# S5 scan: the states of both halves in one tile, both advanced by one VectorE operation, the second half some steps behind

## The chip, the core and the metric

The kernel runs on one core of one Trainium2 chip. Each time is in device microseconds (us) for the whole program. A core has TensorE (PE, matrix products; PEld is its weight load), VectorE (DVE), ScalarE (ACT), GpSimd (POOL) and SyncE (SP, which issues nearly all transfers), and 16 DMA engines that move data between the chip's main memory (DRAM) and its on-chip memory.

## The reference

Two layers over 2048 latent tokens with 256 context tokens in front. The first layer (state space and windowed attention) is not touched. The second is a bidirectional S5 layer: a complex diagonal recurrence along the sequence, with 64 groups of 16 channels, 64 states each, once forwards and once backwards; the context's last state is where the latent part starts.

```python
def s5_scan(u, ab_re, ab_im, bb_re, bb_im, h0_re, h0_im):
    bu_re = jnp.einsum('blgc,gnc->blgn', u, bb_re)
    bu_im = jnp.einsum('blgc,gnc->blgn', u, bb_im)
    ...
    _, _, h_re, h_im = lax.associative_scan(combine, (a_re, a_im, bu_re, bu_im), axis=1)
    return h_re, h_im

def s5_bidir(u, disc, init):
    hf_re, hf_im = s5_scan(u, *disc[0], *init[0])
    hb_re, hb_im = s5_scan(jnp.flip(u, axis=1), *disc[1], *init[1])
    final = [(hf_re[:, -1], hf_im[:, -1]), (hb_re[:, -1], hb_im[:, -1])]
    return hf_re + jnp.flip(hb_re, axis=1), hf_im + jnp.flip(hb_im, axis=1), final

def odd_layer(...):
    u, g = jnp.split(norm_mod(x, norm_w, shift, scale) @ w_in, 2, axis=-1)
    ...
    y = s5_output(s_re, s_im, ug, c_re, c_im, d_skip, glu_w, glu_b) * jax.nn.silu(g)
    x = x + gate * (y @ w_out)
```

## The kernel before

The sequence is cut into 144 blocks of 16 tokens: 16 context blocks, then 128 latent ones. Within a block everything is a matrix product; only the state at the block's edge is carried from block to block. The S5 layer therefore has four parts that run beside each other:

- **odd_proj** (matmuls into tile `mm`, by `mm3` at lines 312 to 314) projects the tokens. Its first blocks give `u`, which goes to DRAM as `u_d` (line 1835), 144 columns per row: 16 of context, 128 of latent. Its later blocks give the gate `g`: ScalarE makes `tz` (line 1849), VectorE `uev` (line 1850). The `mm` tile has two buffers, so TensorE can be at most two tiles ahead of line 1850.
- **s5_in** loads `u_d` (tile `U`, line 1891) and, for each of 64 groups, multiplies it into `ips` (line 1913); ScalarE copies this into `Bu` (lines 1915 and 1916). Groups 0 to 31 are half 0 and fill tile `Bu0`, groups 32 to 63 are half 1 and fill `Bu1`. Each tile is [128, complex part, direction, 16, 145].
- **s5_scan** runs on VectorE alone: 143 steps for each half, each step four dependent operations on 128 x 64 elements (lines 1942, 1943, 1945, 1947), that read and write one slot of `Bu` per state. Forward and backward direction go through the slots in opposite order. Half 0 starts when its input is there; once half 1 has its input too, each step does both halves, eight operations, interleaved. A copy (line 1958) puts the backward start state into slot 144.
- **s5_out** copies the states of a group into `hs` (ScalarE line 1995, forward; GpSimd line 1993, backward) and multiplies (`ops`, lines 2017 and 2019, eight matmuls per group, 512 in all), with `Uo`, `oo` and `ki` loaded from DRAM.

After that **glu** does the last two products. Its first matmuls also run between the last ones of s5_out.

TensorE runs in the order in which the program is written out. A planner (`merge`, `turn`) writes it: it keeps a count `pe` of planned TensorE time, and a generator that yields `("until", t)` or `("wait", x)` is taken up again when `pe` has passed `t`, or `x` is done. The scan charges `SCP` = 0.73 us per half and step, so its pace in that plan fixes where the first matmul of s5_out stands among those of odd_proj. The other engines' order is set by a scheduler; each engine runs its own list in order.

Of the kernel before, what the change touches and what calls it, by code (L numbers as in the profile page):

```python
# [55 lines left out]
def dap(t, off, dims):  # L56
    return bass.AP(tensor=t.tensor, offset=t.offset + off, ap=[list(d) for d in dims])
# [198 lines left out]
class Net:  # L256
# [75 lines left out]
    def scratch(self):  # L332
# [18 lines left out]
        self.x1_d = s("x1_d", [L, D])  # L351
        self.u_d = s("u_d", [64, 16, 16, 144])
        self.g2_d = s("g2_d", [D, LX])
# [1150 lines left out]
    def s5_gen(self, e):  # L1504
# [3 lines left out]
        c = self.const  # L1508
        self.AR = c.tile([P, 2, 32], F32, name="AR")
        self.AI = c.tile([P, 2, 2, 32], F32, name="AI")  # L1510
        cp = e(self.pool("g_c", bufs=1, side="right"))
# [90 lines left out]
        V.tensor_scalar(nq, pw[:, 1, :, :, 8], -1.0, None, op0=ALU.mult)  # L1602
        V.tensor_copy(self.AR, pn[:, 0, 16, :].rearrange("p (a b) -> p a b", a=2))
        V.tensor_scalar(self.AI[:, 0], pn[:, 1, 16, :].rearrange("p (a b) -> p a b", a=2), -1.0, None, op0=ALU.mult)
        V.tensor_copy(self.AI[:, 1], pn[:, 1, 16, :].rearrange("p (a b) -> p a b", a=2))

# [142 lines left out]
    def odd_proj(self):  # L1749
# [69 lines left out]
        def ublk(ch, b):  # L1819
            o = {}  # L1820

            def evac(ci, ps):
                if ci == 0:
                    o["e"] = vp.tile([P, TT], F32, name="uev")
                out = o["e"][:, ci * 256:ci * 256 + ps.shape[-1]]
                if ch[ci] == 0:

                    out = out.rearrange("p (s j) -> p s j", s=16)
                    ps = bass.AP(tensor=ps.tensor, offset=ps.offset + 15, ap=[list(ps.ap[0]), [-1, 16], [16, 16]])
                A.activation(out, ps, AF.Copy)  # L1830

            def end():
                c0, cl = ch[0] == 0, [c for c in ch if c]
                for (q, n, j, S0, j0) in [(0, 16, 16, 0, 0)] * c0 + [(256 * c0, 2 * len(cl), P, 2 * cl[0] - 2, 16) for _ in cl[:1]]:
                    nc.sync.dma_start(dap(self.u_d, b * 8 * 256 * 144 + S0 * 144 + j0, [[16 * 144, P], [144, n], [1, j]]),
                                      o["e"][:, q:q + n * j].rearrange("p (s j) -> p s j", j=j))
# [40 lines left out]
    def s5_in(self, e):  # L1877

        nc = self.nc
        V, G, A, T = nc.vector, nc.gpsimd, nc.scalar, nc.tensor  # L1880
        NJ = 144
        bp = e(self.pool("s5b", bufs=1, side="right"))

        self.Bu = Bu = [bp.tile([P, 2, 2, 16, NJ + 1], F32, name=f"Bu{h}") for h in range(2)]
        self.sp5 = e(self.pool("s5s", bufs=2, side="right"))
        with ExitStack() as st:
            wk = st.enter_context(self.pool("s5i", bufs=2, side="right"))
            pp = st.enter_context(self.pool("s5p", bufs=4, space=PSUM, side="right"))
            def load(g0):
                u = wk.tile([P, 4, 2, NJ], F32, name="U", bufs=3)  # L1890
                nc.sync.dma_start(u.rearrange("p g b t -> p g (b t)"), dap(self.u_d, g0 * 256 * NJ, [[2 * NJ, P], [256 * NJ, 4], [1, 2 * NJ]]))
                return u

            def load_g(g):
# [4 lines left out]
            for g in range(64):  # L1899
                if g % 4 == 0:  # L1900
                    for g0 in ((0, 4) if g == 0 else (g + 4,)):
                        if g0 < 64:
# [8 lines left out]
                for d in range(2):  # L1911
                    for kb in range(2):
                        T.matmul(ps[:, d, :], lhsT=gv[:, d, kb, :], rhs=u[:, g % 4, kb, :], start=kb == 0, stop=kb == 1)
                par = slice((g % 2) * 64, (g % 2) * 64 + 64)
                A.activation(Bu[g // 32][par, 0, :, g // 2 % 16, 0:NJ], ps[0:64], AF.Copy)
                A.activation(Bu[g // 32][par, 1, :, g // 2 % 16, 0:NJ], ps[64:128], AF.Copy)
                if g % 32 == 31:
# [4 lines left out]
    def s5_scan(self):  # L1922

        V, NJ = self.nc.vector, 144
        def slots(k):
            return k, (15 - k if k < 16 else 159 - k)

        def hv(Bu, k, swap=False):
            f, b = slots(k)
            base = Bu[:, 0, 0, :, 0]  # L1930
            W = NJ + 1
            cst = 2 * 16 * W
            part = [list(x) for x in base.ap][0]
            return bass.AP(tensor=base.tensor, offset=base.offset + f + (cst if swap else 0),
                           ap=[part, [-cst if swap else cst, 2], [16 * W + b - f, 2], [W, 16]])
# [12 lines left out]

        k = [1, 1]
        yield ("wait", ("in", 0))  # L1950
        t = self.pe
        while min(k) < NJ:
            w = [h for h in range(2) if k[h] < NJ and ("in", h) in self.done]
            step([(h, k[h]) for h in w])
            for h in w:
                k[h] += 1
                if k[h] == NJ:
                    V.tensor_copy(self.Bu[h][:, :, 1, :, NJ], self.Bu[h][:, :, 1, :, 0])
                    self.done.add(("scan", h))
            t += SCP * len(w)  # L1960
            yield ("until", t)

    def s5_out(self, e):
# [10 lines left out]
        def load(g):  # L1974
            if g % 2 == 0:
                U = wk.tile([P, 2, 2, NJ], F32, name="Uo", bufs=UB)
                nc.sync.dma_start(U.rearrange("p g b t -> p g (b t)"), dap(self.u_d, g * 256 * NJ, [[2 * NJ, P], [256 * NJ, 2], [1, 2 * NJ]]))
                oo = wk.tile([P, 2, 2, 256], F32, name="oo", bufs=UB)
# [21 lines left out]
        for g in range(64):  # L2000
# [245 lines left out]
```

## Time and profile before

| | |
|---|---|
| median of 3 runs | 3734.67 us (3730.95 to 3739.14) |
| the profiled execution: its time, its span | 3735.82 us, 3734.0 us |
| TensorE busy | 3405.1 us, 91% |
| VectorE busy | 2437.0 us, 65% |
| ScalarE, GpSimd busy | 1652.1 us (44%), 1142.7 us (31%) |
| mean granted TensorE clock, share of full | 0.961 |

Busy shares are means over the whole program; what counts for a change is the stage in which it lies. The S5 scan runs from 2919 to 3215 us.

### The profile page before, as it was taken

Reading aid. Unit: us, or ns where it says so; the run is one execution under the profiler, and the core shown is the slowest. Engines: PE = TensorE matmul, PEld = TensorE weight load, DVE = VectorE, ACT = ScalarE, POOL = GpSimd, SP = SyncE. Lnnn points to the kernel's source line nnn. Section 1 sums busy time; section 2 is a strip of 40 time slices with the busy share of each in tenths; the row PEclk is TensorE's granted clock in tenths of the full one; section 3 lists DMA queues with packets and bytes.
Section 4 is the critical chain, followed back from the end, with each engine's and each line's share of the span. In section 5 each row is a group of like instructions: output and inputs, shape, how many; then the busy total and the mean of one; then the engine's idle time right before and its main releaser. Section 6 shows DMA issues by size and latency. Waiting matters only on the chain.

```text
span 3734.0 us, 63256 instructions
## 1 busy us (share of the span) xinstructions
PE 3405.1 (91%) x22805; PEld 2938.9 (79%) x22805; DVE 2437.0 (65%) x5671; ACT 1652.1 (44%) x3567; POOL 1142.7 (31%) x754
## 2 busy tenths in 40 slices
PE   6879899998999998789999999988899979989999
PEld 4767788877887887668778888767688868879977
DVE  5887876565535444767677777798782699404455
ACT  4545445443422222667677775244343512343321
POOL 3221234432212332366676652210101111133121
PEclk9999999999999999899999999999899989989999
DMA  8766477875666776665545443568888844895453
GB/s 291 222 213 196 165 235 251 275 243 192 233 229 220 258 255 213 187 192 148 148 131 137 119 114 110 177 190 255 260 255 271 294 157 165 273 279 169 129 165 113
DMA packets 668004, 758.97 MB, mean 203 GB/s; under 512 B 77147, under 2 KB 529691, under 8 KB 667691
## 3 DMA queue, kind: packets, MB, share of 16 engines
q1 hardware_dynamic: 667691, 754.93, 64.3%
q8 instruction: 180, 2.95, 0.3%
q14 instruction: 133, 1.09, 0.1%
HBM read 517.62 MB, written 237.15 MB: 202 GB/s over the span
## 4 chain that ended last, share of the span: by engine, by line
PE 28%; DVE 13%; DMA 8%; SPq 2%; issue 2%; ACT 2%; POOL 1%; DVEq 0%; ACTq 0%; POOLq 0%
PE pv L1217 3%; PE pt L1207 3%; PE mm L312 2%; PE mm L313 2%; PE mm L314 2%; PE S L1187 2%; PE gpo L312 2%; PE gpo L314 2%; PE gpo L313 2%; DVE sc L1942 1%; PE S L1189 1%; DVE Bu L1947 1%; DVE sc L1945 1%; DVE sc L1943 1%; PE f L312 1%
## 5 line engine op out<-in xcount | busy, mean ns | idle before, releaser
L312 PE MATMUL mm<-xTh,wh 128*128 128x256 f32 (+2 forms) x2344 | 840.1, 358 | 71.1 <-DVE uev L1850 24.7
L313 PE MATMUL mm<-xTl,wh 128*128 128x256 f32 (+2 forms) x2344 | 783.3, 334 | 1.3 <-POOL xTl L297 0.7
L314 PE MATMUL mm<-xTh,wl 128*128 128x256 f32 (+2 forms) x2344 | 783.1, 334 | 0.8 <-DVE wl L297 0.8
L312 PEld LDWEIGHTS mm<-xTh,wh 128*128 128x128 f32 (+1 forms) x2344 | 452.3, 193 | 136.2 <-issue 48.2
L313 PEld LDWEIGHTS mm<-xTl,wh 128*128 128x128 f32 (+1 forms) x2344 | 451.8, 193 | 53.9 <-issue 14.7
L314 PEld LDWEIGHTS mm<-xTh,wl 128*128 128x128 f32 (+1 forms) x2344 | 450.3, 192 | 44.2 <-DVE wl L297 1.0
L1211 DVE TENSOR_TENSOR tl<-pt,th 128x512 fp32r<-128x512 f32 x328 | 224.3, 686 | 117.8 <-ACT th L1210 115.3
L1200 DVE TENSOR_SCALAR_CACHE_REDUCE p<-S,nsink 128x640 f32<-128x640 f32 (+2 forms) x288 | 235.3, 820 | 82.0 <-PE S L1189 79.4
L1201 ACT ACTIVATE p<-p,nm 128x640 f32<-128x640 f32 (+2 forms) x288 | 223.9, 778 | 74.7 <-DVE p L1200 72.7
L1210 ACT ACTIVATE th<-pt 128x512 fp32r<-128x512 f32 x328 | 193.8, 592 | 129.8 <-PE pt L1207 126.2
L1207 PE MATMUL pt<-ident,p 128*128 128x128 f32 x1312 | 203.6, 277 | 36.9 <-DVE tl L1211 16.7
L312 PE MATMUL mm<-wh,xTh 128*128 128x256 f32 x720 | 218.9, 304 | 18.8 <-DMA wh<-wk 9.5
L1207 PEld LDWEIGHTS pt<-ident,p 128*128 128x128 f32 x1312 | 156.8, 142 | 72.1 <-issue 22.2
L313 PE MATMUL mm<-wl,xTh 128*128 128x256 f32 x720 | 207.4, 288 | 0.7 <-DMA wl<-wk 0.7
L314 PE MATMUL mm<-wh,xTl 128*128 128x256 f32 x720 | 207.0, 288 | 0.0
L979 DVE SCALAR_TENSOR_TENSOR rf<-rb,s_P,rf 128x128 f32<-128x128 f32 x288 | 139.2, 528 | 94.2 <-ACT rf L975 90.0
L645 DVE SCALAR_TENSOR_TENSOR cA<-cR,vecs,cA 128x256 f32<-128x256 f32 (+3 forms) x192 | 179.2, 945 | 25.5 <-ACT cA L642 20.9
L424 POOL TENSOR_TENSOR xin<-xin,shr 128x1024 f32<-128x1024 f32 x33 | 86.9, 2641 | 303.1 <-DVE xin L423 298.2
L312 PEld LDWEIGHTS mm<-wh,xTh 128*128 128x128 f32 x720 | 141.7, 197 | 25.8 <-DVE zt L602 10.9
L297 POOL TENSOR_TENSOR wl<-w,wh 128x1024 fp32r<-128x1024 f32 (+1 forms) x43 | 100.3, 2335 | 187.1 <-ACT wh L305 187.0
L911 POOL TENSOR_TENSOR xw<-xs,s_de 128x1024 f32<-128x1024 f32 x36 | 72.1, 2003 | 254.4 <-DMA xs<-xs_d 169.5
L601 ACT ACTIVATE tz<-mm 128x256 f32<-128x256 f32 x144 | 53.9, 377 | 216.1 <-PE mm L314 201.7
(466 smaller groups left out, 9064.9 us busy)
## 6 DMA issues: line engine op xcount, KB each, us to landing
wh<-wk SPq DMA_DIRECT2D x116, 512.0 KB
wl<-wk SPq DMA_DIRECT2D x116, 512.0 KB
wk<-wh SPq DMA_DIRECT2D x56, 512.0 KB
wk<-wl SPq DMA_DIRECT2D x56, 512.0 KB
w<-in_e_w_in_dram SPq DMA_DIRECT2D x40, 512.0 KB
xin<-in_x_dram SPq DMA_DIRECT2D x38, 512.0 KB
rf<-prow_d SPq DMA_DIRECT2D x72, 256.0 KB
rb<-prow_d SPq DMA_DIRECT2D x72, 256.0 KB
```

The lines of the kernel that those rows point to most:

```text
L297: eng.tensor_tensor(out, x, hi.bitcast(F32), ALU.subtract)
L312: mm(ps, lhsT=ah, rhs=bh, start=first, stop=False)
L313: mm(ps, lhsT=ah, rhs=bl, start=False, stop=False)
L314: mm(ps, lhsT=al, rhs=bh, start=False, stop=last)
L645: nc.vector.scalar_tensor_tensor(acc[:, q:q + m], R[:, s + j:s + j + m], cw[:, 12 * j + b:12 * j + b + 1], acc[:, q:q + m], op0=ALU.mult, ...
L979: V.scalar_tensor_tensor(rf[:, h], rb[:, h], self.s_P[:, c, 16 + hh:17 + hh], rf[:, h], op0=ALU.add, op1=ALU.min)
L1200: V.tensor_scalar(p[:, :w], s, -0.125, nsink[:, h:h + 1], op0=ALU.mult, op1=ALU.min, accum_out=nm)
L1201: A.activation(p[:, :w], p[:, :w], AF.Exp, bias=nm, scale=-1.0, accum_out=d["sm"][:, h:h + 1])
L1207: T.transpose(pt[:, n, :], Ps[h4][:, j * P:(j + 1) * P], self.ident)
L1210: A.activation(th, pt, AF.Copy)
L1211: V.tensor_tensor(tl, pt, th.bitcast(F32), ALU.subtract)
L1217: T.matmul(pv, lhsT=VV[kt][:, hk, :], rhs=t.rearrange("p a b -> p (a b)"), start=first and x == 0, stop=last and x == 1)
```

## The change

Both halves' states get one tile `Bu` [128, half, complex part, direction, 16, 144]. The backward direction is stored in the order in which its scan runs, so that both directions stand at slot k in step k: the input matmuls of direction 1 read `U` backwards (step -1 along the row), and the copies of direction 1 into `hs` read `Bu` backwards. For this each row of `u_d` carries the context twice, in front and behind (160 columns, one more transfer for each block of `u`), and `U` is loaded in 32 transfers of two groups instead of 16 of four. The copy into slot 144 is gone. `AR` and `AI` are laid out by half.

The scan has three stretches: half 0 alone until half 1's input is there (`lag` steps), then both in one operation per line, on 128 x 128 elements, with half 1 `lag` slots behind, then half 1 alone. The plan charges a joint step 1.5 x SCP where it charged 2 x SCP.

```diff
-        self.u_d = s("u_d", [64, 16, 16, 144])
+        self.u_d = s("u_d", [64, 16, 16, 160])
...
-                for (q, n, j, S0, j0) in [(0, 16, 16, 0, 0)] * c0 + [(256 * c0, 2 * len(cl), P, 2 * cl[0] - 2, 16) for _ in cl[:1]]:
+                for (q, n, j, S0, j0) in [(0, 16, 16, 0, 0), (0, 16, 16, 0, 144)] * c0 + [(256 * c0, 2 * len(cl), P, 2 * cl[0] - 2, 16) for _ in cl[:1]]:
...
-        self.Bu = Bu = [bp.tile([P, 2, 2, 16, NJ + 1], F32, name=f"Bu{h}") for h in range(2)]
+        self.Bu = Bu = bp.tile([P, 2, 2, 2, 16, NJ], F32, name="Bu")
...
-                u = wk.tile([P, 4, 2, NJ], F32, name="U", bufs=3)
+                u = wk.tile([P, 2, 2, NU], F32, name="U", bufs=4)
...
+            def steps(u, d):
+                return u[:, 0:NJ] if d == 0 else bass.AP(tensor=u.tensor, offset=u.offset + NU - 1, ap=[list(u.ap[0]), [-1, NJ]])
...
-                        T.matmul(ps[:, d, :], lhsT=gv[:, d, kb, :], rhs=u[:, g % 4, kb, :], start=kb == 0, stop=kb == 1)
+                        T.matmul(ps[:, d, :], lhsT=gv[:, d, kb, :], rhs=steps(u[:, g % 2, kb, :], d), start=kb == 0, stop=kb == 1)
...
-        def step(halves):
-            t = {}
-            for h, k in halves:
-                t[h] = [self.sp5.tile([P, 2, 2, 16], F32, name=n, bufs=2) for n in ("sc1", "sc2")]
-                ps = slice(h * 16, h * 16 + 16)
-                V.tensor_tensor(t[h][0], hv(self.Bu[h], k - 1), self.AR[:, None, :, ps].to_broadcast([P, 2, 2, 16]), ALU.mult)
-                V.tensor_tensor(t[h][1], hv(self.Bu[h], k - 1, True), self.AI[:, :, :, ps], ALU.mult)
-            for h, k in halves:
-                V.tensor_tensor(t[h][0], t[h][0], hv(self.Bu[h], k), ALU.add)
-            for h, k in halves:
-                V.tensor_tensor(hv(self.Bu[h], k), t[h][0], t[h][1], ALU.add)
+        def at(h, n, k, lag, swap=False):
+            b = self.Bu[:, h, 0, 0, 0, 0]
+            return bass.AP(tensor=b.tensor, offset=b.offset + k + (C if swap else 0),
+                           ap=[list(b.ap[0]), [-C if swap else C, 2], [2 * C - lag, n], [NJ, 32]])
+
+        def step(h, n, k, lag=0):
+            sh = [P, 2, n, 32]
+            t = [self.sp5.tile([P, 2, 2, 32], F32, name=x, bufs=2)[:, :, 0:n] for x in ("sc1", "sc2")]
+            w = lambda a: a.rearrange("p h d q -> p h (d q)")[:, h:h + n]
+            V.tensor_tensor(t[0], at(h, n, k - 1, lag), w(self.AR)[:, None].to_broadcast(sh), ALU.mult)
+            V.tensor_tensor(t[1], at(h, n, k - 1, lag, True), self.AI.rearrange("p c h d q -> p c h (d q)")[:, :, h:h + n], ALU.mult)
+            V.tensor_tensor(t[0], t[0], at(h, n, k, lag), ALU.add)
+            V.tensor_tensor(at(h, n, k, lag), t[0], t[1], ALU.add)
...
+        t, k = self.pe, 1
+        while k < NJ and ("in", 1) not in self.done:
+            step(0, 1, k)
+            k += 1
+            t += SCP
+            yield ("until", t)
+        yield ("wait", ("in", 1))
+        t = max(t, self.pe - 2.0)
+        lag = k - 1
+        while k < NJ:
+            step(0, 2, k, lag)
+            k += 1
+            t += 1.5 * SCP
+            yield ("until", t)
+        self.done.add(("scan", 0))
+        for k in range(NJ - lag, NJ):
+            step(1, 1, k)
+            t += SCP
+            yield ("until", t)
+        self.done.add(("scan", 1))
...
-                    src = Bu[p0 // 16][par * 64:par * 64 + 64, k, d, p0 % 16, (15, 17)[d]:(15, 17)[d] + P]
+                    src = Bu[par * 64:par * 64 + 64, p0 // 16, k, d, p0 % 16, 15:15 + P]
+                    if d:
+                        src = bass.AP(tensor=src.tensor, offset=src.offset + P - 1, ap=[list(src.ap[0]), [-1, P]])
```

How the change moves instructions: TensorE's order is the same in both kernels up to the place where s5_out begins. Before, that is after 1368 units of odd_proj (a unit is one matmul with 256 columns; one with 512 counts as two), all of them counted from the first matmul of s5_in:

```order
L314 MATMUL mm_33752<-xTh_25428,wl_33472 128x256
L2017 MATMUL ops_33837<-Uo_33812,ki_33816 128x128 x2
L2019 MATMUL ops_33837<-hs_33826,oo_33814 128x128 x2
L2017 MATMUL ops_33837<-Uo_33812,ki_33816 128x128 x2
L2019 MATMUL ops_33837<-hs_33826,oo_33814 128x128 x2
```

In the changed kernel the same matmuls (lines 2030 and 2032 there) stand behind 1152 units, after the `mm` tile 33136:

```order
L314 MATMUL mm_33136<-xTh_25428,wl_32920 128x256
L2030 MATMUL ops_33220<-Uo_33195,ki_33199 128x128 x2
L2032 MATMUL ops_33220<-hs_33209,oo_33197 128x128 x2
L2030 MATMUL ops_33220<-Uo_33195,ki_33199 128x128 x2
L2032 MATMUL ops_33220<-hs_33209,oo_33197 128x128 x2
L2030 MATMUL ops_33237<-Uo_33195,ki_33201 128x128 x2
```

So 216 units have moved from in front of the first matmul of s5_out to behind it. Further on, odd_proj's 1800th and last unit stands after 260 of the 512 s5_out matmuls before, after 312 now.

VectorE's list before, at the last step of half 0 (`Bu0`), with the gate evacuation of `mm` tile 33615 three and a half joint steps ahead of it, and that of tile 33668 right behind one step of half 1 alone:

```order
L1850 SCALAR_TENSOR_TENSOR uev_33640<-tz_33641,mm_33615 128x256
L1945 TENSOR_TENSOR sc1_33723<-sc1_33723,Bu0_30427 128x64
...
L1947 TENSOR_TENSOR Bu0_30427<-sc1_33793,sc2_33794 128x2x2x16
L1947 TENSOR_TENSOR Bu1_30428<-sc1_33797,sc2_33798 128x2x2x16
L1942 TENSOR_TENSOR sc1_33891<-Bu1_30428,AR_25075 128x64
L1943 TENSOR_TENSOR sc2_33892<-Bu1_30428,AI_25076 128x64
L1945 TENSOR_TENSOR sc1_33891<-sc1_33891,Bu1_30428 128x64
L1947 TENSOR_TENSOR Bu1_30428<-sc1_33891,sc2_33892 128x2x2x16
L1850 SCALAR_TENSOR_TENSOR uev_33640<-tz_33717,mm_33668 128x256
```

The same list now, from the evacuation of tile 33136 (the last `mm` tile ahead of s5_out on TensorE) to the first step of half 1 alone; the rows left out are twelve joint steps like those shown:

```order
L1854 SCALAR_TENSOR_TENSOR uev_33161<-tz_33162,mm_33136 128x256
L1949 TENSOR_TENSOR sc1_32951<-sc1_32951,Bu_30435 128x128
L1950 TENSOR_TENSOR Bu_30435<-sc1_32951,sc2_32952 128x2x2x32
...
L1947 TENSOR_TENSOR sc1_33125<-Bu_30435,AR_25075 128x128
L1948 TENSOR_TENSOR sc2_33126<-Bu_30435,AI_25076 128x128
L1949 TENSOR_TENSOR sc1_33125<-sc1_33125,Bu_30435 128x128
L1950 TENSOR_TENSOR Bu_30435<-sc1_33125,sc2_33126 128x2x2x32
L1947 TENSOR_TENSOR sc1_33165<-Bu_30435,AR_25075 128x2x32
```

Before, `mm` tiles 33668 and 33752 still stand on TensorE between the tile that is evacuated last and s5_out; now none does, and thirteen and a half joint steps stand behind that evacuation. Up to the end of half 0's scan there were 66 steps of half 0 alone, 77 joint ones and 43 evacuations by line 1850; now there are 65, 78 and 37. Half 1 alone took 66 steps and takes 65.

## Rows read from the trace of the kernel before

**Rows 1.** Busy time by stretch: start:end, length, then as the header names them.

```profile
core 0: us, PE busy (x) PEld busy (x) DVE busy (x) ACT busy (x) POOL busy (x), PEclk, DMA share, GB/s
2975.00:3000.00 25.00, 17.55 (x85) 14.82 (x84) 24.07 (x110) 5.41 (x14) 2.38 (x1) 0.80 0.70 225
...
3275.00:3300.00 25.00, 16.21 (x93) 15.30 (x94) 2.99 (x3) 11.83 (x22) 8.65 (x13) 0.74 1.03 310
```

**Rows 2.** What TensorE waited for, 2900 to 3260: total us, times, longest.

```profile
PE mm L312 <- DVE uev L1850: 24.7, 12, 7.5
PE tp L431 <- DVE xTl L297: 6.7, 8, 2.0
```

**Rows 3.** VectorE in order of time, one step of half 0 alone: start, us.

```profile
2963.55 0.26 DVE L1942 TENSOR_TENSOR sc<-Bu,AR 128x64 f32<-128x64 f32 x1
2963.73 0.25 DVE L1943 TENSOR_TENSOR sc<-Bu,AI 128x64 f32<-128x64 f32 x1
2963.90 0.26 DVE L1945 TENSOR_TENSOR sc<-sc,Bu 128x64 f32<-128x64 f32 x1
2964.19 0.27 DVE L1947 TENSOR_TENSOR Bu<-sc,sc 128x64 f32<-128x64 f32 x1
2964.50 0.26 DVE L1942 TENSOR_TENSOR sc<-Bu,AR 128x64 f32<-128x64 f32 x1
```

**Rows 4.** VectorE in order of time, a joint step, and one with an evacuation.

```profile
3102.94 0.40 DVE L1947 TENSOR_TENSOR Bu<-sc,sc 128x64 f32<-128x64 f32 x2
3103.25 0.27 DVE L1942 TENSOR_TENSOR sc<-Bu,AR 128x64 f32<-128x64 f32 x1
3103.43 0.26 DVE L1943 TENSOR_TENSOR sc<-Bu,AI 128x64 f32<-128x64 f32 x1
3103.61 0.26 DVE L1942 TENSOR_TENSOR sc<-Bu,AR 128x64 f32<-128x64 f32 x1
3103.78 0.26 DVE L1943 TENSOR_TENSOR sc<-Bu,AI 128x64 f32<-128x64 f32 x1
3103.96 0.45 DVE L1945 TENSOR_TENSOR sc<-sc,Bu 128x64 f32<-128x64 f32 x2
3104.33 0.41 DVE L1947 TENSOR_TENSOR Bu<-sc,sc 128x64 f32<-128x64 f32 x2
3104.63 0.26 DVE L1942 TENSOR_TENSOR sc<-Bu,AR 128x64 f32<-128x64 f32 x1
...
3109.91 0.42 DVE L1850 SCALAR_TENSOR_TENSOR uev<-tz,mm 128x256 f32<-128x256 f32 x1
3110.24 0.27 DVE L1943 TENSOR_TENSOR sc<-Bu,AI 128x64 f32<-128x64 f32 x1
```

**Rows 5.** VectorE operations on rows without gaps, grouped by shape: busy us, mean ns.

```profile
L1336 DVE TENSOR_TENSOR ab<-af,ab 128x64 f32<-128x64 f32 x16 | 3.4, 214 | 2.1 <-PE af L388 2.0
...
L1590 DVE TENSOR_TENSOR pn<-pn,pt 128x128 f32<-128x128 f32 x1 | 0.3, 283 | 0.0
```

**Rows 6.** TensorE in order of time: [idle before it <-releaser].

```profile
2992.10 0.76 PE L312 MATMUL mm<-xTh,wh 128*128 128x512 f32 x1 [7.45 <-DVE uev L1850]
...
3118.04 0.47 PE L312 MATMUL mm<-xTh,wh 128*128 128x512 f32 x1 [0.70 <-DVE uev L1850]
...
3144.91 0.60 PE L2017 MATMUL ops<-Uo,ki 128*128 128x128 f32 x4
3145.35 0.61 PE L2019 MATMUL ops<-hs,oo 128*128 128x128 f32 x4
...
3262.63 0.40 PE L314 MATMUL mm<-xTh,wl 128*128 128x512 f32 x1
...
3359.73 0.61 PE L2019 MATMUL ops<-hs,oo 128*128 128x128 f32 x4
```

**Rows 7.** ScalarE in order of time, where half 0's scan ends.

```profile
3142.97 0.65 ACT L1995 ACTIVATE hs<-Bu 64x128 f32<-64x128 f32 x2 [0.74 <-DVE Bu L1947]
```

**Rows 8.** DMA issues: count and KB each.

```profile
U<-u_d SPq DMA_DIRECT2D x16, 576.0 KB
```

More of the change, by code (lines that the diff above doesn't have):

```diff
@@ L1508, in s5_gen @@
         c = self.const
-        self.AR = c.tile([P, 2, 32], F32, name="AR")
-        self.AI = c.tile([P, 2, 2, 32], F32, name="AI")
+        self.AR = c.tile([P, 2, 2, 16], F32, name="AR")
+        self.AI = c.tile([P, 2, 2, 2, 16], F32, name="AI")
         cp = e(self.pool("g_c", bufs=1, side="right"))
@@ L1602, in s5_gen @@
         V.tensor_scalar(nq, pw[:, 1, :, :, 8], -1.0, None, op0=ALU.mult)
-        V.tensor_copy(self.AR, pn[:, 0, 16, :].rearrange("p (a b) -> p a b", a=2))
-        V.tensor_scalar(self.AI[:, 0], pn[:, 1, 16, :].rearrange("p (a b) -> p a b", a=2), -1.0, None, op0=ALU.mult)
-        V.tensor_copy(self.AI[:, 1], pn[:, 1, 16, :].rearrange("p (a b) -> p a b", a=2))
+        hd = lambda t: t.rearrange("p h d q -> p d h q")
+        a16 = lambda k: pn[:, k, 16, :].rearrange("p (d h q) -> p d h q", d=2, h=2)
+        V.tensor_copy(hd(self.AR), a16(0))
+        V.tensor_scalar(hd(self.AI[:, 0]), a16(1), -1.0, None, op0=ALU.mult)
+        V.tensor_copy(hd(self.AI[:, 1]), a16(1))
         B0 = wk.tile([P, 2, 32, 16], F32, tag="O", name="B0", bufs=4)
@@ L1833, in end @@
                 c0, cl = ch[0] == 0, [c for c in ch if c]
-                for (q, n, j, S0, j0) in [(0, 16, 16, 0, 0)] * c0 + [(256 * c0, 2 * len(cl), P, 2 * cl[0] - 2, 16) for _ in cl[:1]]:
-                    nc.sync.dma_start(dap(self.u_d, b * 8 * 256 * 144 + S0 * 144 + j0, [[16 * 144, P], [144, n], [1, j]]),
+                for (q, n, j, S0, j0) in [(0, 16, 16, 0, 0), (0, 16, 16, 0, 144)] * c0 + [(256 * c0, 2 * len(cl), P, 2 * cl[0] - 2, 16) for _ in cl[:1]]:
+                    nc.sync.dma_start(dap(self.u_d, b * 8 * 256 * 160 + S0 * 160 + j0, [[16 * 160, P], [160, n], [1, j]]),
                                       o["e"][:, q:q + n * j].rearrange("p (s j) -> p s j", j=j))
@@ L1880, in s5_in @@
         V, G, A, T = nc.vector, nc.gpsimd, nc.scalar, nc.tensor
-        NJ = 144
+        NJ, NU = 144, 160
         bp = e(self.pool("s5b", bufs=1, side="right"))
-        self.Bu = Bu = [bp.tile([P, 2, 2, 16, NJ + 1], F32, name=f"Bu{h}") for h in range(2)]
+        self.Bu = Bu = bp.tile([P, 2, 2, 2, 16, NJ], F32, name="Bu")
         self.sp5 = e(self.pool("s5s", bufs=2, side="right"))
@@ L1889, in load @@
             def load(g0):
-                u = wk.tile([P, 4, 2, NJ], F32, name="U", bufs=3)
-                nc.sync.dma_start(u.rearrange("p g b t -> p g (b t)"), dap(self.u_d, g0 * 256 * NJ, [[2 * NJ, P], [256 * NJ, 4], [1, 2 * NJ]]))
-                return u
+                u = wk.tile([P, 2, 2, NU], F32, name="U", bufs=4)
+                nc.sync.dma_start(u.rearrange("p g b t -> p g (b t)"), dap(self.u_d, g0 * 256 * NU, [[2 * NU, P], [256 * NU, 2], [1, 2 * NU]]))
+                return u
+            def steps(u, d):
+                return u[:, 0:NJ] if d == 0 else bass.AP(tensor=u.tensor, offset=u.offset + NU - 1, ap=[list(u.ap[0]), [-1, NJ]])
             def load_g(g):
@@ L1899, in s5_in @@
             for g in range(64):
-                if g % 4 == 0:
-                    for g0 in ((0, 4) if g == 0 else (g + 4,)):
+                if g % 2 == 0:
+                    for g0 in ((0, 2, 4) if g == 0 else (g + 4,)):
                         if g0 < 64:
@@ L1912, in s5_in @@
                     for kb in range(2):
-                        T.matmul(ps[:, d, :], lhsT=gv[:, d, kb, :], rhs=u[:, g % 4, kb, :], start=kb == 0, stop=kb == 1)
+                        T.matmul(ps[:, d, :], lhsT=gv[:, d, kb, :], rhs=steps(u[:, g % 2, kb, :], d), start=kb == 0, stop=kb == 1)
                 par = slice((g % 2) * 64, (g % 2) * 64 + 64)
-                A.activation(Bu[g // 32][par, 0, :, g // 2 % 16, 0:NJ], ps[0:64], AF.Copy)
-                A.activation(Bu[g // 32][par, 1, :, g // 2 % 16, 0:NJ], ps[64:128], AF.Copy)
+                A.activation(Bu[par, g // 32, 0, :, g // 2 % 16], ps[0:64], AF.Copy)
+                A.activation(Bu[par, g // 32, 1, :, g // 2 % 16], ps[64:128], AF.Copy)
                 if g % 32 == 31:
@@ L1924, in s5_scan @@
         V, NJ = self.nc.vector, 144
[L1925 to L1935, printed above, removed]
@@ L1949, in s5_scan @@
-        k = [1, 1]
-        yield ("wait", ("in", 0))
[L1951 to L1960, printed above, removed]
-            yield ("until", t)
+        C = 2 * 16 * NJ
@@ L1975, in load @@
             if g % 2 == 0:
-                U = wk.tile([P, 2, 2, NJ], F32, name="Uo", bufs=UB)
-                nc.sync.dma_start(U.rearrange("p g b t -> p g (b t)"), dap(self.u_d, g * 256 * NJ, [[2 * NJ, P], [256 * NJ, 2], [1, 2 * NJ]]))
+                U = wk.tile([P, 2, 2 * NJ], F32, name="Uo", bufs=UB)
+                nc.sync.dma_start(U, dap(self.u_d, g * 256 * 160 + 16, [[2 * 160, P], [256 * 160, 2], [1, 2 * NJ]]))
                 oo = wk.tile([P, 2, 2, 256], F32, name="oo", bufs=UB)
@@ L2016, in s5_out @@
                 for kb in range(2):
-                    T.matmul(ps[:, tb, :], lhsT=ki[:, kb * 16 + tb * P:kb * 16 + tb * P + P], rhs=U[:, kb, 16:NJ], start=kb == 0, stop=False)
+                    T.matmul(ps[:, tb, :], lhsT=ki[:, kb * 16 + tb * P:kb * 16 + tb * P + P], rhs=U[:, kb * 160:kb * 160 + P], start=kb == 0, stop=False)
                 for d in range(2):
```

## The prediction

> **What bounds the kernel now.** I read the busy shares by stretch first. While the scan runs, VectorE is the full engine: 24.07 of 25 us from 2975 to 3000, against 17.55 us for TensorE, whose granted clock is 0.80 there [rows 1]. The waits say why TensorE has gaps: 24.7 us for line 1850, the evacuation of the gate's products, and 6.7 us for line 297 [rows 2]. Both stand in VectorE's list between scan steps. So until half 0's scan ends, VectorE's list sets the pace, and a scan that cost less there would be worth something. Then the limit changes. ScalarE gets half 0's last needed state at 3142.97 and has the first `hs` at about 3143.6 [rows 7]; TensorE comes to the first matmul of s5_out at 3144.91 and waits for nothing [rows 6]. The two meet within 1.3 us. From there TensorE is full until odd_proj's last matmul (3262.63). Behind that lies a tail in which the transfers are full: share 1.03 at 3275 to 3300, TensorE 16.21 of 25 us, clock 0.74 [rows 1]. Its 252 s5_out matmuls end at about 3360.3: 97.7 us, 0.39 us each, where two took 0.44 us at 3144.91 [rows 6].
>
> **VectorE, part by part.** A step of one half takes 0.95 us from multiply to multiply; its four operations start 0.18, 0.17, 0.29 and 0.31 us apart, so the last two gaps hold about 0.12 us of waiting for the result before [rows 3]. A joint step before is eight operations in 1.38 us, 0.17 each: the other half's work fills those gaps [rows 4]. The new joint step is one chain of four, with the gaps back and 64 more columns per operation. What do 64 more columns cost? No row has a 128 x 128 operation with a step of 144 words. The operation without gaps in its rows takes 214 ns at 64 columns and 283 at 128, so 0.07 us is the lower price [rows 5]. The scan's own operations take 250 to 270 ns at 64 columns [rows 3], about 45 ns more than 214; if that is paid per column, 64 more columns cost 0.07 + 0.045, some 0.115 us. The lowest end of all is nothing, if the operation's time hardly depends on its columns. I take 0.115, since the scan's rows are nearest in kind: 0.95 + 4 x 0.115 = 1.41 us a joint step.
>
> The Trainium skill has a rule that bears on this: the page "Vector Engine (DVE) Microarchitecture Reference", section "5.2 Measured stream behaviour on trn2", gives 1.73 ns per column where one source jumps at every element and 1.054 where all are contiguous. By it, as an estimate, a joint step is 0.95 + 4 x 64 x 1.73 ns = 1.39 us; the rows of the trace say 1.41. It speaks against the change: widening an operation that steps from state to state saves little.
>
> The sum on VectorE up to the end of half 0's scan: one lone step less, -0.95; joint steps 78 x 1.41 = 110.0 against 77 x 1.38 = 106.3, +3.7; six evacuations fewer, at 0.33 each (3109.91 to 3110.24 [rows 4]), -2.0; some twenty of the other 32 now lie in gaps of the chain, where 0.1 us of their time is free, -2.0; the two copies, about -0.4. Together -1.7 us. `hs` is ready at 3143.6 - 1.7 = 3141.9, 3.0 us before 3144.91. A step of 144 words instead of 145 I price at nothing; the bounds are the 45 ns gone or doubled for every 64 columns. Doubled, it is 65 x 4 x 0.045 = 12 us for the lone steps plus 78 x 4 x 0.09 = 28 us for the joint ones, some 40 in all.
>
> **TensorE's order.** This is the larger term. The plan now thinks a joint step costs 1.5 x 0.73 = 1.1 us, and puts s5_out's first matmul 216 units earlier. VectorE's list shows what that means: behind the evacuation of the last `mm` tile ahead of s5_out stand thirteen and a half joint steps, and the first `hs` needs the last but one. So TensorE has finished that tile and then waits for 12.5 steps, 17 us or more, with nothing else in its list. Before, three `mm` tiles covered three and a half such steps. The 216 units took it from 3118.04 to 3144.91, 26.9 us with two waits like the 0.70 shown: 25.4 us of work that now lies behind the wait [rows 6].
>
> After the wait TensorE is the bound again, so what stands there counts fully: 25.4 us, and 52 more s5_out matmuls (312 instead of 260 before odd_proj ends) at 0.22, 11.4 us. The tail loses those 52. At TensorE's price that gives 11.4 back; at the tail's own 0.39 each, 20.2. The transfers bound the tail, but its loads for the last layer stay, so I take the middle, 16. The wait also lowers the clock: after 7.45 us of idleness (to 2992.10) the stretch around it shows 0.80 [rows 1, 6], 5 us of full clock, half of it in the idle time; I add 3.
>
> **The input side.** `U`: 16 loads of 576 KB become 32 of two groups with rows of 320 instead of 288 words, 1/9 more, about 1 MB [rows 8]; at the 310 GB/s of a full stretch [rows 1] that is 3.3 us of transfers, partly covered by matmuls. With the eight short transfers into `u_d` I take 2 us together, bounds 0 and 8. The backward read of `U` I take as free; no row has one. At the worst each of 128 matmuls (144 columns, 0.25 us by the 0.22 for 128) takes twice as long: 32 us, half of it ahead of the scan. The backward copies on GpSimd stay off the path, since `hs` has three buffers.
>
> **Sum.** +25.4 + 11.4 - 16 + 3 - 3.0 + 2 = +22.8 us on the profiled execution's 3735.8 (span 3734.0): 3758.6. That execution lies 1.2 us above the median, so the forecast is 3757. About 0.2% (7.5 us) is what a measurement can tell from no change.
>
> **Rivals.**
> - *Columns cost only their own time* (0.07 us each operation): joint step 0.95 + 0.28 = 1.23 us, 78 x 1.23 = 95.9, 14.1 us less: 3743. For it: rows 5. Against it: the 45 ns that the scan's operations already show.
> - *Faster: the joint step costs no more than a lone one.* An operation's time is then nearly all fixed, the scan has 304 fewer operations in the joint stretch, and a step takes 0.95 us: 74.1, 35.9 less. The first s5_out matmul then runs at about 3106. TensorE could be there, as some 15 of its 24.7 us of waits fall between 2992.10 and 3118.04 and would go. The time is 3757 - 36 = 3721. It decides from a joint step below about 1.02 us (22.8 - 78 x 0.39 = -7.5). For it: a 64-column operation is mostly overhead (214 ns for 64 columns, 283 for twice as many). Against it: that same 0.07 us. The skill's section named above also counts some 75 ns per instruction after overlap, which would make fewer, wider operations pay; the chain's two gaps take most of that back.
> - *No change: the tail gives it all back.* If without the 52 matmuls the transfers no longer bound it, 200 matmuls take 44 us plus some 11 for the last layer's early ones, 42 us less than 97.7 instead of 16: 3757 - 26 = 3731. Against it: the share of 1.03.
> - *Slower still: the new layout reads slowly*, on TensorE (backwards, +16 to +32) or on VectorE (step of 144 words, up to +40): about 3782. No row speaks for or against.
>
> **Chances.** My forecast 0.57, with a range of its own of 3746 to 3770 (tail 11 to 20, input side 0 to 8, clock 2 to 5); columns at their own time 0.14; a joint step as cheap as a lone one 0.11; the tail gives all back 0.05; slow layout 0.13. The range 3731 to 3783 leaves out the faster rival and about half of the slow layout, 0.17. Faster by over 0.2%: the one rival and a little, 0.12. Within 0.2%: the tail and the lower half of the cheap columns, 0.11. Slower: 0.77.
>
> **What the profile after would show.** Line 1947's joint operations at about 0.37 us (0.33 in the first rival, 0.27 in the second) and a joint step near 1.41. TensorE idle for 15 us or more just before the first line 2032, released by `hs`, then a clock at half for some microseconds. The first s5_out matmul at about 3142 plus what the input side adds, odd_proj's last at about 3302, s5_out's last at about 3382. Input matmuls of both directions at the same time apart. I am wrong if TensorE reaches s5_out without that wait, if the joint step is far below 1.4 us, or if the tail shrinks by much more than 16 us.

## The result, and the profile after

The changed kernel takes 3761.15 us (median of 4 runs, 3754.47 to 3765.59) against 3734.96 for the kernel before: ratio 1.0064, 95% interval 1.0047 to 1.0080, slower by some 24 us by the ratio, 26 by the medians. The forecast was 3757. The profiled execution took 3759.46 us, its span is 3757.6 us, 23.6 more than before.

TensorE's waits after (2880 to 3420 us; total us, times, longest), to be read against [rows 2], which end at 3260; up to 3420 the kernel before waits for `hs` twice, 0.7 us at most:

```profile
PE mm L312 <- DVE uev L1854: 21.3, 9, 7.1
PE ops L2032 <- ACT hs L2008: 21.2, 1, 21.2
...
PE tp L432 <- DVE xTl L297: 6.9, 6, 3.4
```

One new row of 21.2 us, a single wait. Its place in TensorE's order of time, with the ends of odd_proj and s5_out, against [rows 6]:

```profile
3123.94 0.28 PE L314 MATMUL mm<-xTh,wl 128*128 128x256 f32 x1
3124.05 0.60 PE L2030 MATMUL ops<-Uo,ki 128*128 128x128 f32 x4
...
3145.89 1.28 PE L2032 MATMUL ops<-hs,oo 128*128 128x128 f32 x4 [21.23 <-ACT hs L2008]
3146.96 1.06 PE L2030 MATMUL ops<-Uo,ki 128*128 128x128 f32 x4
...
3300.52 0.40 PE L314 MATMUL mm<-xTh,wl 128*128 128x512 f32 x1
...
3380.03 0.61 PE L2032 MATMUL ops<-hs,oo 128*128 128x128 f32 x4
```

TensorE is through with its 1152 units at 3124 and has nothing but s5_out next. ScalarE's copy that it waits for starts 2.6 us later on the clock of the program than in [rows 7], since the scan started later:

```profile
3145.53 1.29 ACT L2008 ACTIVATE hs<-Bu 64x128 f32<-64x128 f32 x4 [0.73 <-DVE Bu L1950]
```

After the wait a row of two matmuls (four records) takes 1.06 us instead of 0.60, for some 4 us (at 3150.47 a matmul with 512 columns takes its 0.39 again). The granted clock is 0.54 from 3145.9 to 3150.4, near the lower of its two levels, and 1.00 in the ten us behind; with the idle time in front it is 0.59 (by stretch, columns as in [rows 1]):

```profile
3125.00:3150.00 25.00, 4.11 (x19) 4.11 (x20) 23.70 (x80) 2.85 (x9) 2.48 (x8) 0.59 0.07 26
```

VectorE meanwhile, joint steps against [rows 4]:

```profile
3127.77 0.37 DVE L1947 TENSOR_TENSOR sc<-Bu,AR 128x128 f32<-128x128 f32 x1
3128.06 0.36 DVE L1948 TENSOR_TENSOR sc<-Bu,AI 128x128 f32<-128x128 f32 x1
3128.33 0.37 DVE L1949 TENSOR_TENSOR sc<-sc,Bu 128x128 f32<-128x128 f32 x1
3128.73 0.37 DVE L1950 TENSOR_TENSOR Bu<-sc,sc 128x128 f32<-128x128 f32 x1
3129.14 0.37 DVE L1947 TENSOR_TENSOR sc<-Bu,AR 128x128 f32<-128x128 f32 x1
```

A joint step is 1.37 us, where eight narrow operations took 1.38. The starts are 0.29, 0.27, 0.40 and 0.41 us apart: the fourth operation waits for the third, and the next step for the fourth.

Between the two profiled executions the 23.6 us are found as follows. The scan starts 10.6 us later (2929.45 against 2918.88). From there to the first `hs` matmul it is 216.4 us instead of 226.5, 10.0 less; to ScalarE's copy in front of it, whose own wait ends with VectorE's `Bu`, it is 216.1 instead of 224.1, 8.0 less. The other 2 us are there because TensorE came 2 us after that copy's end before. From that matmul to odd_proj's end it is 155.0 instead of 117.7, 37.4 more. The tail is 79.7 instead of 97.3, 17.6 less, and the rest of the program 3.3 more; another execution of the kernel before (g1) has those 3.3 as well.

### The profile page after: what moved, and what is told of

It reads as the page before. It is cut to its first block, busy times and chain, and to the rows that moved or that the text cites. A ratio compares the mean times of both kernels' runs of the same rounds, so it can differ in the third digit from the quotient of the medians.

```text
span 3757.6 us, 63002 instructions
## 1 busy us (share of the span) xinstructions
PE 3412.2 (91%) x22805; PEld 2943.1 (78%) x22805; DVE 2428.8 (65%) x5357; ACT 1650.4 (44%) x3567; POOL 1143.2 (30%) x754
## 3 DMA queue, kind: packets, MB, share of 16 engines
q14 instruction: 130, 1.06, 0.1%
## 4 chain that ended last, share of the span: by engine, by line
PE 29%; DVE 13%; DMA 7%; SPq 2%; issue 2%; ACT 2%; POOL 1%; DVEq 0%; ACTq 0%; POOLq 0%
PE pv L1218 3%; PE pt L1208 3%; PE mm L312 2%; PE mm L313 2%; PE mm L314 2%; DVE Bu L1950 2%; PE S L1188 2%; DVE sc L1947 2%; PE gpo L312 2%; PE gpo L314 2%; PE gpo L313 2%; PE S L1190 1%; SPq L2094 1%; DVE sc L1949 1%; DVE sc L1948 1%
## 5 line engine op out<-in xcount | busy, mean ns | idle before, releaser
L312 PE MATMUL mm<-xTh,wh 128*128 128x256 f32 (+2 forms) x2344 | 840.4, 359 | 71.6 <-DVE uev L1854 21.3
L1218 PE MATMUL pv<-th,vv 128*128 128x512 f32 x328 | 147.4, 449 | 1.2 <-ACT sA L1150 0.9
```

The lines of the kernel that those rows point to most:

```text
L312: mm(ps, lhsT=ah, rhs=bh, start=first, stop=False)
L1218: T.matmul(pv, lhsT=VV[kt][:, hk, :], rhs=t.rearrange("p a b -> p (a b)"), start=first and x == 0, stop=last and x == 1)
```

## The experiments

Theory: TensorE's order makes the loss. The plan's charge puts s5_out 216 units too early, and TensorE idles. Rivals: the wide operation or the layout is the loss; the input side is. Absolute times differ by some microseconds from one set of runs to the next (the kernel before had medians from 3741 to 3747 us in these sets), so ratios to the kernel before, run beside it, are what counts. In the table "units" are those ahead of s5_out; "wait" is TensorE's for the first `hs`, from the views of waits; "scan" is the time from VectorE's first scan operation to TensorE's first `hs` matmul and "store" that from the first store into `u_d` to the first input matmul, both from the first records of each. Where the wait is 0, "scan" ends with TensorE's arrival and not with the scan: in e8 ScalarE's copy for that matmul starts 217.4 us after the scan's start and in e1 217.9, and TensorE comes 5 and 14 us after its end. All in us but units and ratio.

| run | units | wait | scan | store | ratio, 95% interval |
|---|---|---|---|---|---|
| before, first profile | 1368 | 0 | 226.5 | 272.3 | |
| g1, before again | 1368 | 0 | 227.2 | 270.1 | 1.0001, 0.9990 to 1.0013 |
| e5, before, small U loads | 1368 | 0 | 229.3 | 272.5 | 0.9992, 0.9979 to 1.0005 |
| e6, before, more stores | 1368 | 0 | 228.4 | 280.4 | 1.0011, 0.9998 to 1.0025 |
| e2, before, charge 1.5 | 1128 | 23.6 | 223.2 | 276.8 | 1.0074, 1.0053 to 1.0094 |
| after, first profile | 1152 | 21.2 | 216.4 | 278.4 | 1.0064, 1.0047 to 1.0080 |
| g2, after again | 1152 | 21.2 | 216.7 | 281.5 | 1.0062, 1.0046 to 1.0077 |
| e3, after, eight operations | 1152 | 18.4 | 220.6 | 279.9 | 1.0072, 1.0054 to 1.0091 |
| e7, after, charge 1.8 | 1296 | 3.8 | 218.2 | 279.9 | 1.0010, 0.9999 to 1.0021 |
| e8, after, charge 1.95 | 1368 | 0 | 223.2 | 280.3 | 1.0024, 1.0010 to 1.0037 |
| e1, after, charge 2.0 | 1416 | 0 | 232.3 | 281.3 | 1.0032, 1.0020 to 1.0044 |
| e9, dense, charge 1.5 | 1152 | 14.6 | 190.6 | 283.1 | 0.9982, 0.9969 to 0.9995 |
| f2, dense, eight operations | 1152 | 14.6 | 196.3 | 279.4 | 1.0014, 0.9999 to 1.0029 |
| f1, dense, charge 1.75 | 1272 | 3.6 | 196.1 | 283.6 | 0.9957, 0.9944 to 0.9970 |

### The charge put back in the changed kernel (e1)

```diff
-            t += 1.5 * SCP
+            t += 2.0 * SCP
```

> The changed kernel with one number put back: the plan charges a joint step 2.0 x SCP again. The first s5_out matmul then stands behind 1416 units of odd_proj (1152 in the changed kernel, 1368 before). Layout, wide operations and input side stay as changed. Theory (the plan's pace is the loss): the wait of 21.2 us for the first hs is gone or under 4 us, and what is left over the time before is the input side alone, some 5 to 10 us: 3740 to 3745 us. Rival (the wide operations or the new layout are the loss): nothing comes back, 3755 us or more, and the joint step or the input matmuls show it. Second rival (the tail takes the gain away, as it has 64 matmuls more): 3750 us.

3752.7 us, ratio 1.0032. The wait is gone, and half of the loss with it. The remaining 12 us are more than theory's 5 to 10 and near the second rival, which had s5_out's later place in mind (264 of its matmuls behind odd_proj's end). Its profile shows where the rest lies. The tail is 15 us longer than in the changed kernel (94.9 against 79.7), as that rival says, but no longer than in the kernel before (97.3). Odd_proj ends at 3268.2 and s5_out at 3363.1, 5 and 3 us later than in the first profile before, and from there the program takes 385.2 us instead of 373.7. So most of what it has over the kernel before lies behind s5_out, where no expectation had it; its cause was not tried.

### The charge of the change in the kernel before (e2)

```diff
-            t += SCP * len(w)
+            t += SCP * (0.5 + 0.5 * len(w))
```

> The kernel before with one number changed: the plan charges a joint step 1.5 x SCP instead of 2 x SCP. Scan operations, layout and input side stay as before. The first s5_out matmul moves ahead, behind 1128 units instead of 1368. Theory (the pace is the loss): TensorE waits about 20 us for the first hs, and the time is 3750 to 3757 us, nearly the whole loss of the change. Rival (widening or layout is the loss): 3738 us or less.

Ratio 1.0074: the whole loss, in a kernel with the old layout, narrow operations and old input side. The wait, in TensorE's order of time:

```profile
3160.07 1.22 PE L2019 MATMUL ops<-hs,oo 128*128 128x128 f32 x4 [23.59 <-ACT hs L1995]
```

The one number is enough. The rival that only widening or layout costs falls.

### Eight narrow operations in the changed kernel (e3)

```diff
-            V.tensor_tensor(t[0], at(h, n, k - 1, lag), w(self.AR)[:, None].to_broadcast(sh), ALU.mult)
...
+            for i in range(n):
...
+                kk, hh = k - lag * i, h + i
...
+                V.tensor_tensor(t[0], at(hh, 1, kk - 1, 0), w(self.AR)[:, None].to_broadcast(sh), ALU.mult)
```

(and so for the other three lines.)

> The changed kernel with the joint step done as eight operations on 128 x 64 elements, interleaved as in the kernel before; pace, layout and input side stay as changed, and so does TensorE's order (1152 units). It is the price of one operation for both halves. Theory (neutral: 1.37 us a step either way): 3755 to 3765 us, joint step 1.36 to 1.40 us, hs within 3 us of the changed kernel. Rival (one wide chain of four is slower, as its operations wait for each other): joint step 1.30 us or less, 6 us or more off the wait, about 3754 us. Rival (wide is cheaper where evacuations stand between, as its gaps take them up): 1.45 us or more with the evacuations, 3766 us or more.

Ratio 1.0072 against 1.0064 and 1.0062: the same. A joint step in VectorE's order of time, 3111.95 to 3113.31:

```profile
3111.95 0.26 DVE L1952 TENSOR_TENSOR sc<-Bu,AR 128x64 f32<-128x64 f32 x1
...
3113.31 0.27 DVE L1952 TENSOR_TENSOR sc<-Bu,AR 128x64 f32<-128x64 f32 x1
```

It takes 1.36 us, against 1.37 wide. With all that stands between, the scan is 4.2 us longer (220.6 against 216.4; I had expected at most 3): a joint step with one evacuation in it takes 1.68 us narrow and 1.60 wide (median of 19 each), as the wide chain has gaps in which an evacuation costs less. So widening was worth some 4 us on VectorE, and nothing that these runs can tell in the total.

### The additional stores alone, and the smaller loads alone (e6, e5)

```diff
+                if c0:
+                    nc.sync.dma_start(dap(self.u2_d, b * 8 * 256 * 160 + 144, [[16 * 160, P], [160, 16], [1, 16]]),
+                                      o["e"][:, 0:256].rearrange("p (s j) -> p s j", j=16))
```

> The kernel before with the eight additional small transfers alone (16 context columns of each block of u written a second time, in 64-byte pieces, into a buffer that nobody reads). It tells which part of the input side makes the scan start 10.5 us later in the changed kernel. If it is these transfers: the first input matmul 4 to 6 us later than before, the scan's start 5 us or more later, and the time 3738 to 3742 us. If it is the loads of U in 32 pieces with longer rows: no more than 1 us at the first input matmul, 3735 us.

```diff
-                u = wk.tile([P, 4, 2, NJ], F32, name="U", bufs=3)
+                u = wk.tile([P, 2, 2, NJ], F32, name="U", bufs=4)
```

(with 32 transfers of two groups.)

> The kernel before with U loaded in 32 transfers of two groups with four buffers, as in the changed kernel, rows of 288 words as before. It prices the smaller loads. Theory (free, since the loads stand several groups ahead): ratio within 0.999 to 1.001, time from the first to the last input matmul within 3 us of the kernel before. Rival (part of the rest that is left at 2.0 x SCP): ratio 1.002 or more, with longer waits of the input matmuls.

The loads are free: 0.9992, and from the first to the last input matmul 111.8 us, as before (111.6). The stores delay the first input matmul: counted from the first store into `u_d`, it comes after 270.1 to 276.8 us in the four runs without them and after 278.4 to 283.6 in the ten with them, on average 8 us later (the expectation had 4 to 6). In the total e6 has +0.11%, 4 us, with an interval from nothing to 9 us. Where the delay arises is seen in VectorE's list. In the kernel before:

```profile
2825.98 0.69 DVE L297 TENSOR_TENSOR xTl<-tp,xTh 128x512 fp32r<-128x512 f32 x1 [1.63 <-ACT xTh L472]
2827.13 0.69 DVE L297 TENSOR_TENSOR xTl<-tp,xTh 128x512 fp32r<-128x512 f32 x1 [0.46 <-ACT xTh L472]
2829.89 1.28 DVE L423 SCALAR_TENSOR_TENSOR xin<-xin,rst,scl 128x1024 f32<-128x1024 f32 x1 [2.06 <-DMA xin<-x_d]
```

And in the changed one:

```profile
2826.66 0.69 DVE L297 TENSOR_TENSOR xTl<-tp,xTh 128x512 fp32r<-128x512 f32 x1 [1.63 <-ACT xTh L473]
2830.32 1.29 DVE L424 SCALAR_TENSOR_TENSOR xin<-xin,rst,scl 128x1024 f32<-128x1024 f32 x1 [2.97 <-DMA xin<-x_d]
2831.52 0.68 DVE L297 TENSOR_TENSOR xTl<-tp,xTh 128x512 fp32r<-128x512 f32 x1
```

The second `xTl` has moved behind an operation that waits for a transfer. TensorE waits 3.49 us for it at 2832.26. In e6 it is the same order, with 4.50 us of waiting for the transfer at 2834.17. Counted from the first store, the last of TensorE's `tp` matmuls ahead of that place runs 0.9 us behind the kernel before in the changed one and 0.7 us in e6, the next one 4.6 and 5.9 us behind; the remaining 1.5 and 2.2 us arise after it. Another effect of the stores is made up by then: 14 us after the first one TensorE is 9 us behind in both, as it waits 9 us and more for `wh` instead of 2.0. So the stores cost by what they do to VectorE's list, which a scheduler sets; that is read from the rows, and no run changed that order alone.

### Other charges: the order of before, and one between (e8, e7)

```diff
-            t += 1.5 * SCP
+            t += 1.95 * SCP
```

(1.8 x SCP in e7.)

> The changed kernel with the charge of a joint step at 1.95 x SCP, where TensorE has the order of the kernel before: the first s5_out matmul behind 1368 units, odd_proj's last unit behind 260 s5_out matmuls. What is left of the change is the tile, the wide operations and the input side. Theory (the pace put the loss there; wide operations are neutral; the input side costs about 4 us, as the additional transfers alone did): no wait for hs over 2 us, ratio 1.000 to 1.002. Rival (the rest of the change costs something of its own, as 12 us were left at 2.0 x SCP): ratio 1.003 or more, with odd_proj's end or the tail later than before by that much.

> The changed kernel with the charge at 1.8 x SCP: the first s5_out matmul behind 1296 units. Theory: TensorE, which came to s5_out at 1152 units 21 us too early, comes there some 4 us too early, since 144 units are about 17 us; the time is that of the kernel before within 0.2% on either side. Rival (any s5_out matmul ahead of odd_proj costs, whether TensorE waits or not): about half of the change's loss, ratio 1.003.

With TensorE's order as before the ratio is 1.0024: between theory's 1.000 to 1.002 and the rival's 1.003. It is not decided whether more than the stores is left; the intervals of e6 and e8 overlap. Part of VectorE's gain stays unused in that order: TensorE comes 5 us after the end of the copy into `hs`, where it came 2 us after it in the kernel before. With 1296 units the wait is 3.8 us, as worked out, and the ratio 1.0010, not the 1.003 of the rival. So the order alone makes 15 us (1.0064 against 1.0024) to 20 us (against 1.0010) of the 24, and a place at which TensorE nearly meets the scan has the lowest ratio of the four tried for this layout (the intervals of e7 and e8 overlap).

### A dense order of the words in Bu (e9)

```diff
-        self.Bu = Bu = bp.tile([P, 2, 2, 2, 16, NJ], F32, name="Bu")
+        self.Bu = Bu = bp.tile([P, 2, NJ, 2, 2, 16], F32, name="Bu")
...
-                           ap=[list(b.ap[0]), [-C if swap else C, 2], [2 * C - lag, n], [NJ, 32]])
+                           ap=[list(b.ap[0]), [-C if swap else C, 2], [(NJ - lag) * 64, n], [1, 32]])
```

> The changed kernel with another order of words in Bu: [128, half, slot, complex part, direction, 16], so that a scan operation reads 32 neighbouring words at a time instead of one word in 144; the copies into Bu write, and the copies into hs read, one word in 64. Pace (1.5 x SCP), TensorE's order and input side stay. It prices the columns. Theory (an operation's 45 ns over the 214 ns of a dense one are paid for the stride, per column): wide operation 0.28 us, joint step near 1.05 us, hs 25 us earlier after the scan's start, the wait for hs below 3 us, and a time of 3725 to 3740 us, if the strided copies stay hidden. Rival (the time of a dependent operation does not know the stride): joint step 1.37 us as before, no gain, 3760 us. Rival (ScalarE's strided writes become the limit of s5_in): input matmuls wait for ips buffers, scan starts later, 3750 us or more.

Ratio 0.9982, faster than the kernel before. A joint step in VectorE's order of time:

```profile
3051.47 0.29 DVE L1947 TENSOR_TENSOR sc<-Bu,AR 128x128 f32<-128x128 f32 x1
3051.68 0.28 DVE L1948 TENSOR_TENSOR sc<-Bu,AI 128x128 f32<-128x128 f32 x1
3051.88 0.28 DVE L1949 TENSOR_TENSOR sc<-sc,Bu 128x128 f32<-128x128 f32 x1
3052.20 0.29 DVE L1950 TENSOR_TENSOR Bu<-sc,sc 128x128 f32<-128x128 f32 x1
3052.53 0.29 DVE L1947 TENSOR_TENSOR sc<-Bu,AR 128x128 f32<-128x128 f32 x1
```

1.06 us instead of 1.37; a step of one half is 0.79 us (2960.47 to 2961.26) instead of 0.95. The scan to the first `hs` is 25.8 us shorter, as forecast. The wait was to fall below 3 us, and is 14.6: TensorE gained too, as its waits for line 1854 fell from 21.3 to 10.6 us and its granted clock, from the scan's start to its wait, rose from 0.94 to 0.98; it came to s5_out 19 us sooner after the scan's start. ScalarE pays for it:

```profile
L1925 ACT ACTIVATE Bu<-ips 64x288 f32<-64x288 f32 x64 | 43.1, 674 | 0.8
```

674 ns a copy where the changed kernel took 406. That stays hidden for the most part: 116.4 us from the first to the last input matmul, against 115.6 and 111.7 in the two profiles of the changed kernel.

### Eight operations in the dense order (f2), and a fitting charge (f1)

The edits are those of e3 on e9, and 1.75 x SCP on e9.

> The changed kernel with the dense order of words in Bu and the joint step as eight operations on 128 x 64 elements, at the changed pace (1.5 x SCP, 1152 units). It asks whether one operation for both halves is worth more where a column costs less. Theory (an operation in the dense layout starts 0.14 us after the one before it if nothing is waited for): eight take 1.10 to 1.16 us against 1.06 for the four wide ones, 3 to 8 us more to the first hs, a wait of 18 to 22 us, ratio 0.999 to 1.001. Rival (the narrow operations fill the gaps of the chain entirely, so that widening is worth nothing in either layout): 1.06 us or less, and a wait and a ratio as with four.

> The changed kernel with the dense order of words in Bu (as in the run of that layout) and the charge of a joint step at 1.75 x SCP: the first s5_out matmul behind 1272 units instead of 1152. With the dense layout TensorE still waited 14.6 us for the first hs at 1152 units, and 120 units are about 14 us of work. Theory (the order has to fit the scan as it runs): the wait falls below 3 us, the scan takes the same time to the first hs within 3 us, and the ratio to the kernel before is 0.993 to 0.996, faster than either kernel. Rival (with the scan so short TensorE's order no longer matters, since other limits come next): 0.998 as at 1.5 x SCP.

Eight narrow operations, VectorE's order of time:

```profile
3084.18 0.21 DVE L1952 TENSOR_TENSOR sc<-Bu,AR 128x64 f32<-128x64 f32 x1
3084.32 0.21 DVE L1953 TENSOR_TENSOR sc<-Bu,AI 128x64 f32<-128x64 f32 x1
...
3085.27 0.21 DVE L1952 TENSOR_TENSOR sc<-Bu,AR 128x64 f32<-128x64 f32 x1
```

A step of 1.09 us against 1.06, and 5.7 us more to the first `hs`; the ratio 1.0014 is worse than e9's 0.9982, and its wait (expected at 18 to 22) is no longer, since TensorE came later as well. So here one operation for both halves has a value; the ratios lie 12 us apart, about twice what the scan shows, and what makes the other half is not read from any row.

The charge of 1.75 brings 0.9957: faster than either kernel by 0.4% and 1.1%. What is left of the wait, expected below 3 us, in the view of waits:

```profile
PE ops L2032 <- ACT hs L2008: 3.6, 1, 3.6
```

The scan is 5.5 us longer than in e9, more than the 3 that I allowed; 42 evacuations of odd_proj stand ahead of its end now, 37 in e9.

### Both kernels again, side by side (g1, g2)

> The kernel before, unchanged, profiled again. In the profiles shown first, the first input matmul came at 2864.5 us before and at 2870.4 in the changed kernel; in every other run of this study, with the old or the new input side, it came at 2872 to 2884. Theory (that place differs from execution to execution, and the 5.9 us are no price of the change): here too it comes at 2870 us or later. Rival (the additional transfers and smaller loads make the delay): 2866 us or earlier.

> The changed kernel, unchanged, on the same chip as the run of the kernel before beside it. Theory: from the scan's start to the first hs 216 us within 3, a wait for hs of 18 to 24 us, ratio 1.005 to 1.008. If the input side costs what the first profiles showed, its first input matmul comes 4 us or more later than in that run; if not, within 3 us on either side.

The kernel before has its first input matmul at 2876.4 here, the changed one at 2879.2; g2's wait is 21.2 us, its scan 216.7, its ratio 1.0062. So where this stage starts differs by 12 us between two executions of the same kernel, and the 5.9 us between the first two profiles could not be read as a price. The interval from the first store on, which leaves out what lies ahead, shows one (272.3 and 270.1 against 278.4 and 281.5).

## Why the prediction was right

The forecast sum was +22.8 us, the spans differ by 23.6. That they agree to 1 us is in part luck: the scan's start moved by +10.6 us, where I had +2, and the stretch from there to the first `hs` matmul by -10.0, where I had -3.0, and the two errors cancel. The larger terms, those behind the wait, were right by themselves. By its steps:

- **VectorE's price of a wide operation.** Forecast 0.37 us and a joint step of 1.41; measured 0.36 to 0.37 and 1.37 in the step shown (median of the 44 without other work: 1.39). The choice between the bounds was right: the strided price, not the dense one, and the rival "as cheap as a lone one" (0.95) falls. The step of 144 words costs nothing against 145: a step of one half stays at 0.94 us (2975.60 to 2976.54).
- **The first `hs`.** Forecast 1.7 us less on VectorE's list, which makes `hs` ready 3.0 us before TensorE came to it, and +2 from the input side. Both were mis-sized, in opposite directions. VectorE's list became 8.0 us shorter up to the copy into `hs` (224.1 to 216.1); the other 2 of the 10.0 are TensorE's later arrival before. Of the 8.0, e2, with the earlier order alone and seven evacuations fewer, has 1.3 (222.8); e3 against the changed kernel gives 4.2 for the wide operations, where I had a loss of 3.7 - 2.0; and e3 against e2 leaves 2.6 for layout, lag and copies, which no run parts. The input side came to some 8 us by the interval from the first store, as I priced the stores by their transfers and not by what moves in VectorE's list; my bound was 8. So the first `hs` matmul came at 3145.89, where I had put the first s5_out matmul at 3142 plus the input side.
- **Work behind the wait.** Forecast 25.4 + 11.4 + 3 = 39.8; measured 37.4 from the first `hs` matmul to odd_proj's end (3300.5, forecast 3302). Right, and e2 has it with one number changed. I had put the wait at 17 us or more; it was 21.2.
- **The tail.** Forecast -16 within 11.4 to 20.2; measured -17.6, and -20.3 in the pair g1, g2. That size is less sure than the pairs say: e5 and e6, in the order of before, have tails of 90.2 and 89.6 us instead of 97. The rival that the tail gives all back (-42) falls.
- **Reading U backwards.** Forecast free; the input matmuls have the same durations in both kernels (283 and 286 ns, lowest and median; 286 in the median for either direction).

So the mechanism was the one forecast. What I did not see is in the rival on dense columns: it gave the wide operation its dense price without a dense layout. The page "Vector Engine (DVE) Microarchitecture Reference" of the Trainium skill, section "5.2 Measured stream behaviour on trn2", whose 1.73 and 1.054 ns per column I had quoted, says the same as these runs: from 64 to 128 columns an operation grows by 0.11 us strided (0.26 to 0.37), 1.7 ns a column, and by 0.065 dense (0.22 to 0.285), 1.0 ns.

Open: whether the 0.24% that e8 keeps over the kernel before is more than the additional stores, and whether an order of VectorE's list as before would take their price away. That was not tried.

## What to carry to other kernels

Where a planner sets one engine's order by a charge for another engine's work, that charge is part of the change: a joint step that took as long as before, but was charged a quarter less, cost 15 to 20 us here. Before widening a dependent chain, look at what its gaps are filled with and at how its words lie: widening alone gave 4 us, neighbouring words 26 us, and the total moved only as far as the waiting engine's order was fitted to it. Between two profiles compare stretches that begin at a mark of their own, since a stage may start 12 us earlier or later in two executions of the same kernel.

## What the runs showed of the hardware

- Neighbouring words: the same 128 x 64 operation takes 0.22 us instead of 0.26, the 128 x 128 one 0.285 instead of 0.37, and the chain's gap shrinks with it (0.32 to 0.33 us from one dependent operation's start to the next, instead of 0.40 to 0.41).
- ScalarE pays for strided words as well: 64 x 288 elements written one word in 64 took 674 ns instead of 406; `hs` copies of 128 columns that read one word in 64 took 427 instead of 309 (GpSimd's 422 instead of 318).
- SP's queue, in e6 (count: lowest, median, highest ns of an issue): the eight additional stores (line 1839, 2048 pieces of 64 bytes each) held it 3.5 us in the median. It is not the pieces alone: eight of the stores of line 1836 write such pieces too and held it 0.5 to 1.9 us, those with pieces of 512 bytes mostly 0.39. The five additional stores that were issued within 0.1 us of the end of such a store's issue held it 3.2 to 5.1 us, the three that came 2 us or more after it 0.5 to 0.6.

```profile
L1836 SPq DMA_DIRECT2D u_d<-uev x29: 365/385/1897, 2594.5 to 2890.0; - x29
L1839 SPq DMA_DIRECT2D u_d<-uev x8: 518/3476/5074, 2597.7 to 2688.4; - x8
```
